# Hybrid decoder layer in fp32 on one core: half 0's seven-product stages with rounded part and remainder side by side

## The chip, the cores and the metric

The kernel runs on one core of a Trainium2 chip. The metric is the device time of one execution in microseconds; lower is better. The median of three runs of the kernel before is 2952.33 us (2952.29 to 2953.47).

## What is computed

One layer of a hybrid decoder trunk, for 1024 prompt tokens and 64 sample tokens of width 1024: two half-step SwiGLU feed-forward networks (FFN1, FFN2) around a token mixer (a pooling branch and a Mamba-2 SSD branch, merged by gates), then a final norm. All in fp32.

```
def swiglu(x, w_in, w_out):
    gu = x @ w_in
    g, u = gu[..., :D_FF], gu[..., D_FF:]
    return (jax.nn.silu(g) * u) @ w_out

x = x + 0.5 * swiglu(rmsnorm(x, norm_ffn1), ffn1_w_in, ffn1_w_out)
mix, ... = token_mixing(rmsnorm(x, norm_mix), ...)
x = x + mix
x = x + 0.5 * swiglu(rmsnorm(x, norm_ffn2), ffn2_w_in, ffn2_w_out)
```

D_MODEL is 1024 and D_FF is 2816. The change concerns `x @ w_in` of both FFNs.

## The kernel before

Tokens lie along the columns and channels on the 128 partitions. They are split into half 0 (512 tokens) and half 1 (576 tokens, the samples among them). An fp32 product is made from three products of a rounded type (fp32r): an operand is split into its rounded part (`hi`, `xh`, `wh`) and the remainder (`lo`, `xl`, `wl`), and wh·xh + wh·xl + wl·xh is summed in PSUM. ScalarE rounds, VectorE subtracts (`split`, L350 and L352 for activations; L455 and L456, or L289 and L290, for weights).

**Input product of an FFN.** It goes through 22 blocks `ff` of 128 channels of g and 128 of u. The first blocks (3 for half 0, 2 for half 1: `N_PLAIN`) are made plainly. The others (`ffn_in`, `wino`) use a Strassen-Winograd scheme: g and u for two groups of tokens are a 2 x 2 block product over two halves of the 1024 input channels, which takes seven products rather than eight. Each product has 4 K tiles of 128 and a width of 256 columns in half 0 or 288 in half 1. `combine` makes its operands: those of products 1, 2 and 3 are slices of the normed, split tiles `hi` and `lo`; those of 4 to 7 are sums, split by `put` (tiles `X`, the rounded part in columns 0 to n, the remainder next to it; for product 4 into a part of `hi` and `lo` that is no longer used). `wino_weights` makes the seven weight operands: four raw tiles, four sums s1 to s4 on GpSimd (L449), each split into wh and wl.

The products run in the order 1, 2, 6, 5, 7, 3, 4 and gather in three PSUM banks a half: A takes 1, 6, 7, 4 (each added to what lies there), B takes 2, C takes 5 and 3. `after` takes out what is needed after each product, with ScalarE copies (L548, L556, L558), VectorE adds (L553, L560, L562) and a multiply (L565), two SiLUs on ScalarE (L554, L563) and a multiply on GpSimd (L566). There are six such banks, so the next block's A, B and C are the same banks. In blocks 3 to 20 each product is made for half 0 and then for half 1 with the same weights ("joint" blocks, 18 in each FFN); block 2 is half 1's alone; block 21 (`N_APART`) is made for half 0 alone and then for half 1 alone. The result of a block is stored to DRAM (`hd`, L567).

**Output product.** For each half the 22 stored tiles come back (`hr`, L629), are split into `hh` and `hr`, and are multiplied with `w_out` in 8 blocks of output channels (`po`). All 22 tiles stay in SBUF for the half.

**What sets the order.** The program is written as generators that are stepped by due times on a model clock of TensorE; a tile framework adds the waits and chooses the order on each engine by priority. Weight splits and sums have a raised priority (`hp`). SyncE issues nearly all DMAs, in order: a load whose buffer is not free holds back those behind it. Activation tiles of [128, 576] come from a pool of 58 (`act`) and, in the FFNs, from one of 17 (`fx`).

Of the kernel before, what the change touches and what calls it, by code (L numbers as in the profile page):

```python
# [8 lines left out]
F32 = mybir.dt.float32  # L9
# [5 lines left out]
P = 128  # L15
# [47 lines left out]
def tile_hybrid_pool_ssd_macaron(  # L63
# [340 lines left out]
    def norm_split(xt, h, gi, out, pace=1.0):  # L404

        N = NTOK[h]
        rr = []
        yield from rstd(xt, h, D, rr, pace)
        hi, lo = [], []
        for k in range(KD):  # L410
            a = act((P, N), F32R, "hi")
            b = act((P, N), F32R, "lo")
            t = act((P, N), name="xn")
            V.tensor_tensor(t, xt[k], rr[0], op=ALU.mult)
            split(t, a, b, cols[:, gi + k : gi + k + 1])
            hi.append(a)
            lo.append(b)
            yield pace
        out.append((h, hi, lo))
# [59 lines left out]
    def wino(weights, nk, xs, after):  # L479


        banks = [[None] * 3 for _ in xs]
        for (p, b), (wh, wl) in zip(PRODUCTS, weights):
            for i, (h, X) in enumerate(xs):
                n = NPAIR[h]
                new = banks[i][b] is None
                if new:
                    banks[i][b] = psum("pd", "pw" + p)
                out = banks[i][b][:, :n]
                for k in range(nk):  # L490
                    xh, xl = X[p][k]
                    for j, (W, x) in enumerate(((wh, xh), (wh, xl), (wl, xh))):
                        mm(out, W[:, k, :], x, start=new and k == 0 and j == 0, stop=k == nk - 1 and j == 2, free=True)
                after(p, i, banks[i])
                tick()

    def combine(h, xn, hi, lo, X, pace):

        n = NPAIR[h]
        f, s_ = slice(0, n), slice(n, 2 * n)
        X["1"] = [(hi[i][:, f], lo[i][:, f]) for i in range(4)]
        X["2"] = [(hi[4 + i][:, f], lo[4 + i][:, f]) for i in range(4)]
        X["3"] = [(hi[4 + i][:, s_], lo[4 + i][:, s_]) for i in range(4)]
        for p in "6574":
            X[p] = []

        def sub(out, a, b):
            G.tensor_tensor(out, a, b, op=ALU.subtract)  # L510

        def put(src, p, a=None, b=None):
            if a is None:
                t = act((P, 576), F32R, "X")
                a, b = t[:, f], t[:, s_]
            S.activation(a, src, AF.Copy)
            V.tensor_tensor(b, src, a.bitcast(F32), op=ALU.subtract)
            X[p].append((a, b))

        for i in range(4):  # L520
            a, b = xn[i], xn[4 + i]
            sub(a[:, s_], a[:, s_], a[:, f])
            t2 = fx(name="t2")[:, f]
            sub(t2, b[:, s_], a[:, s_])
            put(t2, "6")
            put(a[:, s_], "5")
            yield pace
            sub(a[:, f], t2, a[:, f])
            sub(b[:, f], b[:, f], t2)
            put(a[:, f], "7")  # L530
            yield pace
        yield None
        for i in range(4):
            put(xn[4 + i][:, f], "4", hi[i][:, s_], lo[i][:, s_])
            yield pace

    def ffn_in(wi, ff, xs):

        out = {}

        def after(p, i, bk):
            h = xs[i][0]
            n = NPAIR[h]
            A, B, C = (b[:, :n] if b is not None else None for b in bk)
            if p == "1":
                t = fx(name="t")
                out[i] = o = {"g": fx(name="g"), "t1": t[:, :n], "t5": t[:, :n], "t2": t[:, n : 2 * n]}
                S.copy(o["t1"], A)  # L548
                return
            o = out[i]  # L550
            g1, g2 = o["g"][:, :n], o["g"][:, n : 2 * n]
            if p == "2":
                V.tensor_tensor(g1, B, o["t1"], op=ALU.add)  # L553
                S.activation(g1, g1, AF.Silu)  # L554
            elif p == "6":
                S.copy(o["t2"], A)  # L556
            elif p == "5":
                S.copy(o["t5"], C)  # L558
            elif p == "7":
                V.tensor_tensor(o["t5"], A, o["t5"], op=ALU.add)  # L560
            elif p == "3":
                V.tensor_tensor(g2, C, o["t2"], op=ALU.add)  # L562
                S.activation(g2, g2, AF.Silu)  # L563
            else:
                V.tensor_tensor(g1, g1, A, op=ALU.mult)  # L565
                G.tensor_tensor(g2, g2, o["t5"], op=ALU.mult)  # L566
                dma(hdram[h][ff], o["g"][:, : 2 * n])  # L567

        wino(wino_weights(wi, 0, 4, 4, ff * P, FF + ff * P), 4, xs, after)
# [17 lines left out]
    def ffn(wi, wo, prep, after, half=None, side=None):  # L587
# [33 lines left out]
        for h in HALVES:  # L621
            N = NTOK[h]
            parts = [], []
            for k in range(NFF):

                own = k < 4 if h == 0 else not half and k >= NFF - 2
                t, a = (fx(d, n_) if own else act((P, 576), d, n_) for d, n_ in ((F32, "hr"), (F32R, "hh")))
                t = t[:, :N]
                dma(t, hdram[h][k])  # L629
                split(t, a[:, :N], t.bitcast(F32R))  # L630
# [35 lines left out]
    def load_x(h, out):  # L666
# [37 lines left out]
        hi, lo, xn = [None] * KD, [None] * KD, [None] * KD  # L704
        for k in range(KD):
            pt = psum("ps", "ptx")
            for i in range(4):
                mm(pt[:, i * P : (i + 1) * P], raws[i][k // 4][:, (k % 4) * P : (k % 4 + 1) * P], dg[i])
            x = fx(name="xn") if k >= 4 else act((P, 576), name="xn")
            a, b = act((P, 576), F32R, "hi"), act((P, 576), F32R, "lo")  # L710
            g = cols[:, i_g1 + k : i_g1 + k + 1]
            S.activation(x[:, :512], pt, AF.Copy, scale=g)
            V.tensor_scalar_mul(a[:, :512], pt, g)
# [5 lines left out]
            hi[k], lo[k], xn[k] = a, b, x  # L719
            yield 0.9  # L720
        out.append((h, hi, lo, xn))

    def turn_x(h):

# [15 lines left out]
    def norm_parts(xt, h, gi, out, pace=1.0):  # L740

        N = NTOK[h]
        rr = []
        yield from rstd([t[:, :N] for t in xt], h, D, rr, pace)
        hi, lo, xn = [], [], []
        for k in range(KD):
            x = fx(name="xn") if k >= 4 else act((P, 576), name="xn")
            a, b = act((P, 576), F32R, "hi"), act((P, 576), F32R, "lo")
# [6 lines left out]
        out.append((h, hi, lo, xn))  # L755


    ch, hn = {}, []
# [798 lines left out]
```

## Time and profile before

| | |
|---|---|
| median of three runs | 2952.33 us |
| span of the profiled execution | 2950.3 us (its own time lies some 2.0 us above, taken from the median) |
| TensorE busy | 2900.3 us (98%), 19740 matmuls |
| VectorE / ScalarE / GpSimd busy | 1646.5 us (56%) / 1187.0 us (40%) / 445.1 us (15%) |
| matmuls of half 0's seven-product blocks (`pw`, 256 columns) | 608 x 3 on `hi`, `lo`; 912 + 456 on `X` |
| FFN1's seven-product stage | about 106 to 529 us of the span |

In a profile row the engine, the line, the operation and the tiles (out<-in) are followed by the shape; groups have count, busy time in us, mean ns of one, and the idle time ahead with what ended it. A window row has its bounds, its length, busy us and count of PE, PEld, DVE, ACT and POOL, then the granted clock, the DMA share and GB/s. PE is TensorE, DVE VectorE, ACT ScalarE, POOL GpSimd, SP SyncE.

### The profile page before, as it was taken

Reading aid. Unit: us, or ns where it says so; the run is one execution under the profiler, and the core shown is the slowest. Engines: PE = TensorE matmul, PEld = TensorE weight load, DVE = VectorE, ACT = ScalarE, POOL = GpSimd, SP = SyncE. Lnnn points to the kernel's source line nnn. Section 1 sums busy time; section 2 is a strip of 40 time slices with the busy share of each in tenths; the row PEclk is TensorE's granted clock in tenths of the full one; section 3 lists DMA queues with packets and bytes.
Section 4 is the critical chain, followed back from the end, with each engine's and each line's share of the span. In section 5 each row is a group of like instructions: output and inputs, shape, how many; then the busy total and the mean of one; then the engine's idle time right before and its main releaser. Section 6 shows DMA issues by size and latency. Waiting matters only on the chain. (4 is left out here: it accounts for less than half of the span.)

```text
span 2950.3 us, 52088 instructions
## 1 busy us (share of the span) xinstructions
PE 2900.3 (98%) x19740; PEld 2689.1 (91%) x19740; DVE 1646.5 (56%) x3134; ACT 1187.0 (40%) x2418; POOL 445.1 (15%) x528
## 2 busy tenths in 40 slices
PE   7999999999999999999999999999999999999998
PEld 6999999789988888788999988999999999997898
DVE  5654445434273897777633776867665443443432
ACT  5444444333242665443332454442333433342322
POOL 5433333000000000000000010100034333330000
PEclk9999999999999999999999999999999999999999
DMA  4465554864335888678434566556574522236652
GB/s 131 155 220 176 164 161 152 271 201 142 101 98 168 276 258 265 196 225 286 118 97 152 170 184 183 168 155 186 178 240 155 165 90 76 79 106 203 197 179 72
DMA packets 542273, 501.36 MB, mean 170 GB/s; under 512 B 36388, under 2 KB 391780, under 8 KB 542014
## 3 DMA queue, kind: packets, MB, share of 16 engines
q1 hardware_dynamic: 542006, 498.03, 54.0%
q8 instruction: 155, 2.54, 0.4%
q14 instruction: 96, 0.79, 0.1%
q10 hardware_dynamic: 16, 0.00, 0.0%
HBM read 355.94 MB, written 142.20 MB: 169 GB/s over the span
## 5 line engine op out<-in xcount | busy, mean ns | idle before, releaser
L290 DVE TENSOR_TENSOR wl<-wraw,wh 128x512 fp32r<-128x512 f32 (+1 forms) x416 | 282.8, 681 | 394.7 <-ACT wh L289 386.6
L289 ACT ACTIVATE wh<-wraw 128x512 fp32r<-128x512 f32 (+1 forms) x416 | 256.4, 617 | 603.0 <-PE po L161 233.7
L161 PE MATMUL pw<-hi,wh 128*128 128x288 f32 (+1 forms) x1248 | 361.3, 289 | 2.6 <-DVE t L560 2.2
L161 PE MATMUL pw<-hi,wl 128*128 128x288 f32 (+1 forms) x1248 | 360.1, 289 | 0.0
L161 PE MATMUL pw<-lo,wh 128*128 128x288 f32 (+1 forms) x1248 | 359.9, 288 | 0.0
L161 PE MATMUL pw<-X,wh 128*128 128x288 f32 (+1 forms) x1872 | 356.9, 289 | 0.2 <-ACT t L556 0.2
L161 PEld LDWEIGHTS pw<-X,wh 128*128 128x128 f32 x1872 | 295.8, 190 | 0.4 <-ACT t L556 0.4
L161 PE MATMUL po<-hh,wh 128*128 128x288 f32 (+1 forms) x1056 | 288.1, 330 | 6.8 <-ACT hh L350 6.6
L161 PE MATMUL po<-hr,wh 128*128 128x288 f32 (+1 forms) x1056 | 289.4, 328 | 0.0
L161 PE MATMUL po<-hh,wl 128*128 128x288 f32 (+1 forms) x1056 | 288.6, 328 | 0.0
L161 PE MATMUL pw<-X,wl 128*128 128x288 f32 (+1 forms) x936 | 270.1, 289 | 0.0
L161 PEld LDWEIGHTS pw<-hi,wh 128*128 128x128 f32 x1248 | 236.2, 189 | 3.5 <-DVE t L560 2.6
L161 PEld LDWEIGHTS pw<-lo,wh 128*128 128x128 f32 x1248 | 236.1, 189 | 0.0
L161 PEld LDWEIGHTS pw<-hi,wl 128*128 128x128 f32 x1248 | 236.1, 189 | 0.0
L456 DVE TENSOR_TENSOR wl<-s,wh 128x512 fp32r<-128x512 f32 x168 | 123.4, 736 | 145.3 <-ACT wh L455 142.2
L161 PEld LDWEIGHTS po<-hh,wh 128*128 128x128 f32 x1056 | 179.0, 189 | 24.3 <-ACT hh L350 11.1
L161 PEld LDWEIGHTS po<-hr,wh 128*128 128x128 f32 x1056 | 179.9, 189 | 15.8 <-DVE hr L352 2.3
L161 PEld LDWEIGHTS po<-hh,wl 128*128 128x128 f32 x1056 | 180.0, 189 | 14.2 <-DMA wl<-part 0.4
L161 PEld LDWEIGHTS pw<-X,wl 128*128 128x128 f32 x936 | 178.1, 190 | 0.0
L455 ACT ACTIVATE wh<-s 128x512 fp32r<-128x512 f32 x168 | 106.2, 632 | 174.4 <-PE pw L161 170.7
L161 PE MATMUL pc<-hi,wh 128*128 128x288 f32 (+1 forms) x576 | 161.5, 334 | 0.0
L161 PE MATMUL pc<-lo,wh 128*128 128x288 f32 (+1 forms) x576 | 158.2, 328 | 0.0
(341 smaller groups left out, 6391.0 us busy)
## 6 DMA issues: line engine op xcount, KB each, us to landing
wh<-part SPq DMA_DIRECT2D x204, 256.0 KB
wl<-part SPq DMA_DIRECT2D x204, 256.0 KB
wraw<-in_ffn_w_in_dram SPq DMA_DIRECT2D x188, 256.0 KB
wraw<-in_w_in_dram SPq DMA_DIRECT2D x180, 256.0 KB
wraw<-in_ffn_w_out_dram SPq DMA_DIRECT2D x120, 256.0 KB
part<-wh SPq DMA_DIRECT2D x112, 256.0 KB
part<-wl SPq DMA_DIRECT2D x112, 256.0 KB
ab<-acsd SPq DMA_DIRECT2D x64, 256.0 KB
```

The costliest lines, as they stand in the source:

```text
L161: T.matmul(out, lhsT, rhs, start=start, stop=stop, skip_group_check=free)
L289: S.activation(wh, raw, AF.Copy)
L290: V.tensor_tensor(wl, raw, wh.bitcast(F32), op=ALU.subtract)
L455: S.activation(wh, a, AF.Copy)
L456: V.tensor_tensor(wl, a, wh.bitcast(F32), op=ALU.subtract)
```

## The change

Half 0's operands get a layout in which the rounded part and the remainder lie in one tile: `pair` gives [128, 2, 576], eight of them, and the pool of act tiles shrinks from 58 to 42. `X` tiles are read as two pieces of 256 columns. For half 0, `wino` makes per K tile one matmul of 512 columns with wh on both pieces, into a whole bank, and one of 256 with wl on the rounded part, into the bank's first half. The two halves of a bank are thus two parts of one sum; `after0` takes them out side by side (copies and adds of 512 columns) and sums them on GpSimd (`halves`), or for product 4 with a ScalarE copy of the second half and a VectorE add. A third fx tile `v` is used per block. Half 1 is computed as before. The pairs also hold the mixer norm's `hi` and `lo` (`norm_split`) and, in the output stage, tiles 4 to 11 of half 0 (and of half 1 in FFN2).

```diff
...
 PIECES = (((0, 512),), ((0, 288), (288, 576)), ((0, 256),), ((256, 576),))
 HALF_OF = (0, 1, 1, 1)
 NPAIR = (256, 288)
-N_ACT, N_BIG, N_PD = 58, 3, 4
+N_ACT, N_PAIR, N_BIG, N_PD = 42, 8, 3, 4
 N_RAW, N_W = 6, 3
 N_FX, N_S, N_PDF = 17, 4, 6
 N_PLAIN, N_APART = (3, 2), 1
...
     def act(shape=(P, 576), dt=F32, name="a"):
         return sp.tile(list(shape), dt, tag="act", bufs=N_ACT, name=nm(name))
+    def pair(n, name="hl"):
+        t = sp.tile([P, 2, 576], F32R, tag="pair", bufs=N_PAIR, name=nm(name))
+        return t[:, 0, :n], t[:, 1, :n], t
     stage = {}
...
         yield from rstd(xt, h, D, rr, pace)
         hi, lo = [], []
         for k in range(KD):
-            a = act((P, N), F32R, "hi")
-            b = act((P, N), F32R, "lo")
+            a, b, _ = pair(N)
             t = act((P, N), name="xn")
             V.tensor_tensor(t, xt[k], rr[0], op=ALU.mult)
             split(t, a, b, cols[:, gi + k : gi + k + 1])
...
                 if new:
                     banks[i][b] = psum("pd", "pw" + p)
                 out = banks[i][b][:, :n]
+                if h == 0:
+                    both = banks[i][b].rearrange("p (a b) -> p a b", a=2)
+                    for k in range(nk):
+                        x = X[p][k]
+                        mm(both, wh[:, k, :], x, start=new and k == 0, stop=False, free=True)
+                        mm(out, wl[:, k, :], x[:, 0, :], start=False, stop=k == nk - 1, free=True)
+                    after(p, i, banks[i])
+                    tick()
+                    continue
                 for k in range(nk):
                     xh, xl = X[p][k]
                     for j, (W, x) in enumerate(((wh, xh), (wh, xl), (wl, xh))):
...
                 after(p, i, banks[i])
                 tick()
-    def combine(h, xn, hi, lo, X, pace):
+    def combine(h, xn, hi, lo, hl, X, pace):
         n = NPAIR[h]
         f, s_ = slice(0, n), slice(n, 2 * n)
-        X["1"] = [(hi[i][:, f], lo[i][:, f]) for i in range(4)]
-        X["2"] = [(hi[4 + i][:, f], lo[4 + i][:, f]) for i in range(4)]
-        X["3"] = [(hi[4 + i][:, s_], lo[4 + i][:, s_]) for i in range(4)]
+        for p, i0, cs in (("1", 0, f), ("2", 4, f), ("3", 4, s_)):
+            X[p] = [(hi[i0 + i][:, cs], lo[i0 + i][:, cs]) if h else hl[i0 + i][:, :, cs] for i in range(4)]
         for p in "6574":
             X[p] = []
...
             G.tensor_tensor(out, a, b, op=ALU.subtract)
         def put(src, p, a=None, b=None):
+            both = None
             if a is None:
                 t = act((P, 576), F32R, "X")
                 a, b = t[:, f], t[:, s_]
+                both = t[:, : 2 * n].rearrange("p (a b) -> p a b", a=2)
             S.activation(a, src, AF.Copy)
             V.tensor_tensor(b, src, a.bitcast(F32), op=ALU.subtract)
-            X[p].append((a, b))
+            X[p].append((a, b) if h else both)
         for i in range(4):
             a, b = xn[i], xn[4 + i]
...
         yield None
         for i in range(4):
             put(xn[4 + i][:, f], "4", hi[i][:, s_], lo[i][:, s_])
+            if h == 0:
+                X["4"][i] = hl[i][:, :, s_]
             yield pace
     def ffn_in(wi, ff, xs):
         out = {}
+
+        def after0(p, i, bk):
+
+            A, B, C = bk
+            n = NPAIR[0]
+            f, s_ = slice(0, n), slice(n, 2 * n)
+            if p == "1":
+                out[i] = o = {"g": fx(name="g"), "t": fx(name="t"), "v": fx(name="v")}
+                S.copy(o["t"][:, : 2 * n], A)
+                return
+            g, t, v = out[i]["g"], out[i]["t"], out[i]["v"]
+
+            def halves(o, x):
+                G.tensor_tensor(o, x[:, f], x[:, s_], op=ALU.add)
+
+            if p == "2":
+                V.tensor_tensor(g[:, : 2 * n], B, t[:, : 2 * n], op=ALU.add)
+                halves(g[:, f], g)
+                S.activation(g[:, f], g[:, f], AF.Silu)
+            elif p == "6":
+                S.copy(v[:, : 2 * n], A)
+            elif p == "5":
+                S.copy(t[:, : 2 * n], C)
+            elif p == "7":
+                V.tensor_tensor(t[:, : 2 * n], A, t[:, : 2 * n], op=ALU.add)
+                halves(t[:, f], t)
+            elif p == "3":
+                V.tensor_tensor(v[:, : 2 * n], C, v[:, : 2 * n], op=ALU.add)
+                halves(g[:, s_], v)
+                S.activation(g[:, s_], g[:, s_], AF.Silu)
+            else:
+                S.copy(t[:, s_], A[:, s_])
+                V.tensor_tensor(t[:, s_], A[:, f], t[:, s_], op=ALU.add)
+                V.tensor_tensor(g[:, f], g[:, f], t[:, s_], op=ALU.mult)
+                G.tensor_tensor(g[:, s_], g[:, s_], t[:, f], op=ALU.mult)
+                dma(hdram[0][ff], g[:, : 2 * n])
         def after(p, i, bk):
             h = xs[i][0]
+            if h == 0:
+                return after0(p, i, bk)
             n = NPAIR[h]
             A, B, C = (b[:, :n] if b is not None else None for b in bk)
             if p == "1":
...
         for h in HALVES:
             finish(prep[h][0])
             x = prep[h][1][0]
-            gen = combine(h, x[3], x[1], x[2], X[h], T_PACE)
+            gen = combine(h, x[3], x[1], x[2], x[4], X[h], T_PACE)
             def first(gen):
                 for p in gen:
...
             for k in range(NFF):
                 own = k < 4 if h == 0 else not half and k >= NFF - 2
-                t, a = (fx(d, n_) if own else act((P, 576), d, n_) for d, n_ in ((F32, "hr"), (F32R, "hh")))
+                if 4 <= k < 4 + N_PAIR and (h == 0 or half):
+                    a, t, _ = pair(576, "hp")
+                    t = t.bitcast(F32)
+                else:
+                    t, a = (fx(d, n_) if own else act((P, 576), d, n_) for d, n_ in ((F32, "hr"), (F32R, "hh")))
                 t = t[:, :N]
                 dma(t, hdram[h][k])
                 split(t, a[:, :N], t.bitcast(F32R))
...
         N = NTOK[h]
         rr = []
         yield from rstd([t[:, :N] for t in xt], h, D, rr, pace)
-        hi, lo, xn = [], [], []
+        hi, lo, xn, hl = [], [], [], []
         for k in range(KD):
             x = fx(name="xn") if k >= 4 else act((P, 576), name="xn")
-            a, b = act((P, 576), F32R, "hi"), act((P, 576), F32R, "lo")
+            a, b, both = (act((P, 576), F32R, "hi"), act((P, 576), F32R, "lo"), None) if h else pair(576)
             V.scalar_tensor_tensor(x[:, :N], xt[k][:, :N], cols[:, gi + k : gi + k + 1], rr[0], op0=ALU.mult, op1=ALU.mult)
             split(x[:, :N], a[:, :N], b[:, :N])
             hi.append(a)
             lo.append(b)
             xn.append(x)
+            hl.append(both)
             yield pace
     ch, hn = {}, []
```

In the rows below, a name is followed by its tile's number. **TensorE, product 1 of half 0 in a joint block of FFN1, and the first matmuls of half 1.** Before:

```order
L161 MATMUL pw1_579_3118<-hi_46_281,wh_577_3114 128x256
L161 MATMUL pw1_579_3118<-lo_47_282,wh_577_3114 128x256
L161 MATMUL pw1_579_3118<-hi_46_281,wl_578_3115 128x256
L161 MATMUL pw1_579_3118<-hi_50_292,wh_577_3114 128x256
L161 MATMUL pw1_579_3118<-lo_51_293,wh_577_3114 128x256
L161 MATMUL pw1_579_3118<-hi_50_292,wl_578_3115 128x256
L161 MATMUL pw1_579_3118<-hi_54_303,wh_577_3114 128x256
L161 MATMUL pw1_579_3118<-lo_55_304,wh_577_3114 128x256
L161 MATMUL pw1_579_3118<-hi_54_303,wl_578_3115 128x256
L161 MATMUL pw1_579_3118<-hi_58_314,wh_577_3114 128x256
L161 MATMUL pw1_579_3118<-lo_59_315,wh_577_3114 128x256
L161 MATMUL pw1_579_3118<-hi_58_314,wl_578_3115 128x256
```

After:

```order
L164 MATMUL pw1_588_2998<-hl_46_281,wh_586_2994 128x512
L164 MATMUL pw1_588_2998<-hl_46_281,wl_587_2995 128x256
L164 MATMUL pw1_588_2998<-hl_49_291,wh_586_2994 128x512
L164 MATMUL pw1_588_2998<-hl_49_291,wl_587_2995 128x256
L164 MATMUL pw1_588_2998<-hl_52_301,wh_586_2994 128x512
L164 MATMUL pw1_588_2998<-hl_52_301,wl_587_2995 128x256
L164 MATMUL pw1_588_2998<-hl_55_311,wh_586_2994 128x512
L164 MATMUL pw1_588_2998<-hl_55_311,wl_587_2995 128x256
L164 MATMUL pw1_592_3011<-hi_89_437,wh_586_2994 128x288
```

Of three matmuls for each K tile two are left, the first of 512 columns; half 1 follows as before.

**ScalarE at the boundary between two joint blocks** (`wh` are weight splits of the next block's first products; `g` SiLUs; `pw1` is bank A, `pw5` bank C). Before:

```order
L455 ACTIVATE wh_577_3114<-wraw_573_3106 128x512
L563 ACTIVATE g_531_2837<-g_531_2837 128x256
L455 ACTIVATE wh_585_3154<-wraw_574_3108 128x512
L563 ACTIVATE g_534_2853<-g_534_2853 128x288
L455 ACTIVATE wh_596_3199<-s2_595_3197 128x512
L735 COPY xr_465_2514<-ptr_571_3095 128x64
L735 COPY xr_467_2516<-ptr_571_3095 128x64
L548 COPY t_580_3131<-pw1_579_3118 128x256
L455 ACTIVATE wh_598_3229<-s1_594_3195 128x512
L548 COPY t_583_3147<-pw1_582_3134 128x288
```

After:

```order
L457 ACTIVATE wh_586_2994<-wraw_582_2986 128x512
L353 ACTIVATE ph_577_2979<-pr_574_2931 128x512
L457 ACTIVATE wh_595_3027<-wraw_583_2988 128x512
L583 ACTIVATE g_537_2745<-g_537_2745 128x256
L615 ACTIVATE g_542_2763<-g_542_2763 128x288
L585 COPY t_538_2746<-pw1_536_2736 128x256
L457 ACTIVATE wh_602_3064<-s2_601_3062 128x512
L562 COPY t_590_3008<-pw1_588_2998 128x512
```

Between half 1's SiLU (L615) and the copy for product 1 of the next block (L562) there is now a copy of a part of bank A after product 4 (L585). On VectorE an add and a multiply (L586, L587) stand where the multiply L565 stood.

**GpSimd over the same block** (`s1` to `s4` are weight sums of the next block). Before:

```order
L449 TENSOR_TENSOR s1_594_3195<-wraw_575_3110,wraw_576_3112 128x512
L449 TENSOR_TENSOR s2_595_3197<-s1_594_3195,wraw_573_3106 128x512
L449 TENSOR_TENSOR s3_603_3263<-wraw_573_3106,wraw_575_3110 128x512
L449 TENSOR_TENSOR s4_611_3302<-wraw_574_3108,s2_595_3197 128x512
L566 TENSOR_TENSOR g_531_2837<-g_531_2837,t_530_2836 128x256
L566 TENSOR_TENSOR g_534_2853<-g_534_2853,t_533_2852 128x288
```

After:

```order
L451 TENSOR_TENSOR s1_600_3060<-wraw_584_2990,wraw_585_2992 128x512
L451 TENSOR_TENSOR s2_601_3062<-s1_600_3060,wraw_582_2986 128x512
L567 TENSOR_TENSOR g_537_2745<-g_537_2745 128x256
L451 TENSOR_TENSOR s3_613_3125<-wraw_582_2986,wraw_584_2990 128x512
L451 TENSOR_TENSOR s4_617_3156<-wraw_583_2988,s2_601_3062 128x512
L567 TENSOR_TENSOR t_538_2746<-t_538_2746 128x256
L567 TENSOR_TENSOR g_537_2745<-v_539_2747 128x256
L588 TENSOR_TENSOR g_537_2745<-g_537_2745,t_538_2746 128x256
L618 TENSOR_TENSOR g_542_2763<-g_542_2763,t_541_2762 128x288
```

The three sums of bank halves (L567) stand between the weight sums and ahead of the closing multiplies (L588, L618).

**SyncE at the transition from FFN1's input to its output product** (`hr` and `hp` loads of stored tiles, whose number follows `hd0_`; `wh`, `wl` weights; `hd0_21`, `hd1_21` the stores of the last blocks). Before, from tile 8 of half 0 on:

```order
L629 DMA hr_1188_6607<-hd0_8_129 128x512
L629 DMA hr_1172_6567<-hd0_0_121 128x512
L629 DMA hr_1190_6612<-hd0_9_130 128x512
L629 DMA hr_1174_6572<-hd0_1_122 128x512
L279 DMA wh_1220_6695<-part_436_2309 128x512
L629 DMA hr_1192_6617<-hd0_10_131 128x512
L629 DMA hr_1176_6577<-hd0_2_123 128x512
L279 DMA wl_1221_6697<-part_438_2310 128x512
L279 DMA wh_1224_6727<-part_455_2427 128x512
L567 DMA hd1_21_164<-g_1153_6449 128x576
L629 DMA hr_1178_6582<-hd0_3_124 128x512
L629 DMA hr_1194_6622<-hd0_11_132 128x512
```

After, from tile 8 on:

```order
L685 DMA hp_1195_6177<-hd0_8_129 128x512
L685 DMA hp_1196_6181<-hd0_9_130 128x512
L589 DMA hd0_21_142<-g_1135_5896 128x512
L685 DMA hr_1183_6141<-hd0_0_121 128x512
L685 DMA hp_1197_6185<-hd0_10_131 128x512
L685 DMA hp_1198_6189<-hd0_11_132 128x512
L685 DMA hr_1205_6208<-hd0_15_136 128x512
L282 DMA wl_1226_6279<-part_319_1645 128x512
L685 DMA hr_1185_6146<-hd0_1_122 128x512
L282 DMA wh_1223_6261<-part_425_2182 128x512
L685 DMA hr_1207_6213<-hd0_16_137 128x512
L282 DMA wl_1224_6263<-part_427_2183 128x512
```

And on to tile 3:

```order
L685 DMA hr_1187_6151<-hd0_2_123 128x512
L282 DMA wh_1227_6293<-part_444_2279 128x512
L619 DMA hd1_21_164<-g_1164_6023 128x576
L685 DMA hr_1209_6218<-hd0_17_138 128x512
L685 DMA hr_1189_6156<-hd0_3_124 128x512
```

Tiles 4 to 9 (in the pairs) stand ahead of tile 0, and tiles 15, 16 and 17 have come between tiles 0 and 3. The number of DMAs is the same.

More of the change, by code (lines that the diff above doesn't have):

```diff
@@ L718, in load_x @@
             (G if k % 2 else V).tensor_tensor(b[:, :N], x[:, :N], a[:, :N].bitcast(F32), op=ALU.subtract)
-            hi[k], lo[k], xn[k] = a, b, x
+            hi[k], lo[k], xn[k], hl[k] = a, b, x, both
             yield 0.9
-        out.append((h, hi, lo, xn))
+        out.append((h, hi, lo, xn, hl))
     def turn_x(h):
@@ L744, in norm_parts @@
         yield from rstd([t[:, :N] for t in xt], h, D, rr, pace)
-        hi, lo, xn = [], [], []
+        hi, lo, xn, hl = [], [], [], []
         for k in range(KD):
             x = fx(name="xn") if k >= 4 else act((P, 576), name="xn")
-            a, b = act((P, 576), F32R, "hi"), act((P, 576), F32R, "lo")
+            a, b, both = (act((P, 576), F32R, "hi"), act((P, 576), F32R, "lo"), None) if h else pair(576)
             V.scalar_tensor_tensor(x[:, :N], xt[k][:, :N], cols[:, gi + k : gi + k + 1], rr[0], op0=ALU.mult, op1=ALU.mult)
@@ L753, in norm_parts @@
             xn.append(x)
+            hl.append(both)
             yield pace
-        out.append((h, hi, lo, xn))
+        out.append((h, hi, lo, xn, hl))
     ch, hn = {}, []
```

2 lines of the change are left out of this document (1 added, 1 removed).

## The prediction

> **What bounds the kernel now.** I read the page first, then the waits of TensorE, the windows over the seven-product stage, the groups by shape, and last the timeline at the places that the change touches. From the page:
>
> ```profile
> span 2950.3 us, 52088 instructions
> PE 2900.3 (98%) x19740; PEld 2689.1 (91%) x19740; DVE 1646.5 (56%) x3134; ACT 1187.0 (40%) x2418; POOL 445.1 (15%) x528
> ```
>
> TensorE is busy for 98% of the span, and no other engine for more than 56%. Some 2.0 us of the 2952.33 us median lie around this span, so sums made against the span can be put on the median. The seven-product stage of FFN1 in one window, and TensorE's longest waits that lie at the change:
>
> ```profile
> 106.00:506.00 400.00, 399.79 (x3175) 399.09 (x3175) 199.44 (x358) 177.76 (x395) 139.81 (x113) 1.00 0.55 175
> PE po L161 <- ACT hh L350: 6.6, 7, 1.8
> PE pw L161 <- DVE t L560: 2.2, 2, 1.1
> ```
>
> In 400 us TensorE stands still for 0.2 us, at a granted clock of 1.00; VectorE is busy for half of it, ScalarE for 44%, GpSimd for 35%. So in this stage time goes down only when TensorE's own stream gets shorter, and up only when a new wait appears. The waits of the output product `po` (6.6 us) lie at the transition to it, and the 2.2 us of `pw` are two stalls in the block that half 0 has for itself.
>
> **The merged matmuls (the gain).** What is removed:
>
> ```profile
> L161 PE MATMUL pw<-hi,wh 128*128 128x256 f32 x608 | 172.3, 283 | 2.2 <-DVE t L560 2.2
> L161 PE MATMUL pw<-hi,wl 128*128 128x256 f32 x608 | 171.7, 282 | 0.0
> L161 PE MATMUL pw<-X,wh 128*128 128x256 f32 x912 | 168.9, 283 | 0.0
> L161 PE MATMUL pw<-X,wl 128*128 128x256 f32 x456 | 129.0, 283 | 0.0
> ```
>
> The mean of one is a latency, for neighbours overlap; the price is the distance between starts. Half 0 has 38 blocks of 7 products of 4 K tiles: 1064 K tiles (608 on norm tiles and 456 on `X` tiles, as the counts show), each with two 256-column matmuls on `wh`. These two become one of 512 columns, so 1064 matmuls go, each with its weight load. Starts from the timeline: two whole half-0 products (12 matmuls of 256 columns each, up to the first of half 1), the next block's first matmul, and 512-column matmuls of the output stage, 23 steps apart.
>
> ```profile
> 312.81 0.28 PE L161 MATMUL pw<-hi,wh 128*128 128x256 f32 x1
> ...
> 314.23 0.30 PE L161 MATMUL pw<-hi,wh 128*128 128x288 f32 x1
> ...
> 315.83 0.28 PE L161 MATMUL pw<-hi,wh 128*128 128x256 f32 x1
> ...
> 318.83 0.28 PE L161 MATMUL pw<-hi,wh 128*128 128x256 f32 x1
> ...
> 320.27 0.30 PE L161 MATMUL pw<-hi,wh 128*128 128x288 f32 x1
> ...
> 2674.68 0.39 PE L161 MATMUL po<-hh,wl 128*128 128x512 f32 x1
> ...
> 2679.89 0.39 PE L161 MATMUL po<-hr,wh 128*128 128x512 f32 x1
> ```
>
> A product takes 314.23 - 312.81 = 1.42 or 320.27 - 318.83 = 1.44 us, so a 256-column matmul 118 to 120 ns. A 512-column one takes 5.21 / 23 = 226.5 ns. A merge saves 2 x 118.3 - 226.5 = 10 to 2 x 120 - 226.5 = 13.5 ns, which is 10.7 to 14.4 us for 1064; I take 12.5 ns (most steps in the timeline are 120): **-13.3 us**. The 512-column row has one contiguous operand and the new one reads two 256-column pieces that lie 576 columns apart (for `X` they touch). No row shows such a read; a gain from it is excluded, and the loss reaches from nothing to the whole saving. I take nothing, since the rows price a matmul by its columns: 288 of them cost (315.83 - 314.23) / 12 = 133 ns, above 256 by what the columns say.
>
> Here the Trainium skill speaks against the change: the page "TensorE: Matmul & The Clock Gate", section "Back-to-back issue gap", gives a warm gap of N / 2.4 + 2.5 ns, so only 2.5 ns are fixed per matmul and the merges would bring an estimated 2.7 us. The rows put the fixed part at some 12 ns (120 ns at 256 columns, 226.5 at 512), and I go by them.
>
> **Leaving PSUM.** Per half-0 block ScalarE's three copies and VectorE's two adds double in width, ScalarE and VectorE get one more 256-column operation each, and GpSimd three adds of 256 columns. Nearest rows, and GpSimd's multiply of the same size:
>
> ```profile
> L548 ACT COPY t<-pw 128x256 f32<-128x256 f32 x38 | 14.1, 372 | 28.3 <-PE pw L161 28.1
> L815 ACT COPY craw<-pc 128x512 f32<-128x512 f32 x24 | 13.8, 576 | 0.1
> L560 DVE TENSOR_TENSOR t<-pw,t 128x256 f32<-128x256 f32 x38 | 16.0, 422 | 4.2 <-PE pw L161 3.5
> L1264 DVE TENSOR_TENSOR hst<-hst,pst 128x512 f32<-128x512 f32 x28 | 19.1, 681 | 0.7 <-PE pst L161 0.3
> 312.37 0.74 POOL L566 TENSOR_TENSOR g<-g,t 128x256 f32<-128x256 f32 x1 [5.17 <-ACT g L563]
> ```
>
> ScalarE gets 3 x (576 - 372) + 372 = 984 ns more per block, VectorE 3 x (681 - 422) + 422 = 1.2 us (its third add was in width 256 too), GpSimd 3 x 0.74 = 2.2 us. A joint block lasts 7 x (1.42 + 1.60) = 21 us, of which each is busy for half or less, so their sums cost nothing; only latency to TensorE's next use of a bank can. Banks: A is written by products 1, 6, 7, 4 in this order, C by 5 and 3, B by 2. In between, each copy has the other half's product and two more (1.6 + 1.4 + 1.6 us or so), against 0.58 or 0.68 for the operation. The tight one is bank A after product 4: only half 1's product 4 (1.60 us) lies before the next block writes A. Before, one multiply frees it:
>
> ```profile
> 314.02 0.93 POOL L566 TENSOR_TENSOR g<-g,t 128x288 f32<-128x288 f32 x1 [0.91 <-ACT g L563]
> 314.43 0.42 DVE L565 TENSOR_TENSOR g<-g,pw 128x256 f32<-128x256 f32 x1 [0.15 <-PE pw L161]
> ```
>
> It ends at 314.85, 0.98 us ahead of 315.83. After, a copy (0.37) and an add (0.42) stand in its place, with a handover of about 0.15 between engines (the idle in the row above): 314.43 + 0.37 + 0.15 + 0.42 = 315.37, 0.46 us ahead. GpSimd's 0.93 us ran beside this VectorE operation without stretching it. ScalarE holds two SiLUs and a weight split ahead of the copy, and the first SiLU now waits for GpSimd's sum; from product 3's end I count 0.15 + 0.68 (add) + 0.74 (sum), then 0.63 + 0.42 + 0.45 on ScalarE, which is 3.1 us, just where product 4 ends (1.60 + 1.40). So I put **0** here, with 0.4 us of cover.
>
> **Half 0's own block** (the last in each FFN). With no half-1 products between, a product is 1.4 us away from the next use of its bank. Before, it lost 1.1 us ahead of product 4:
>
> ```profile
> 507.90 1.29 POOL L449 TENSOR_TENSOR s<-wraw,wraw 128x512 f32<-128x512 f32 x1 [2.52 <-DVE wl L456]
> 509.89 1.30 POOL L449 TENSOR_TENSOR s<-s,wraw 128x512 f32<-128x512 f32 x1 [0.70 <-DVE wl L456]
> 516.13 0.39 PE L161 MATMUL pw<-hi,wh 128*128 128x256 f32 x1 [1.08 <-DVE t L560]
> ```
>
> After, GpSimd's first sum stands behind the two weight sums of the next block, which end at 511.19. Then follow the sum 0.74, the SiLU 0.42, a weight split 0.63 and the copy of A 0.58 on ScalarE: 513.6, while product 7 could begin at about 506.3 + 4 x 1.38 = 511.8. That is a stall of 1.8 us in place of one of about 1.1 to 1.2, which then has time to pass unseen: +0.6 us for each FFN, bounds 0 and +2, together **+1.2**.
>
> **Transition to the output product.** SyncE issues loads in order. Tiles 4 to 11 of half 0 now lie in the pairs and so can be loaded only when products 3 and 4 of half 0's last block are done, and six of them stand ahead of tile 0; tiles 12 to 17 come ahead of tile 3. In the trace tile 3 is what TensorE waits for:
>
> ```profile
> 529.61 0.32 SPq L567 DMA_DIRECT2D hd<-g  x1
> 529.98 0.93 SPq L629 DMA_DIRECT2D hr<-hd  x2
> 535.33 0.50 PE L161 MATMUL po<-hh,wh 128*128 128x512 f32 x1 [1.64 <-ACT hh L350]
> 2666.89 0.80 PE L161 MATMUL po<-hh,wh 128*128 128x512 f32 x2 [1.84 <-ACT hh L350]
> 523.00:526.00 3.00, 3.00 (x24) 2.93 (x24) 2.62 (x5) 2.74 (x7) 0.00 (x0) 1.00 0.53 192
> 526.00:529.00 3.00, 3.00 (x24) 3.00 (x24) 2.07 (x5) 1.42 (x3) 0.37 (x1) 1.00 0.67 226
> 532.00:535.00 3.00, 1.70 (x8) 1.04 (x6) 0.00 (x0) 0.35 (x1) 0.00 (x0) 1.00 0.86 278
> 2660.60:2671.20 10.60, 8.76 (x31) 6.27 (x30) 3.78 (x6) 2.68 (x5) 0.58 (x2) 0.84 0.91 296
> ```
>
> The load of tile 3 is issued behind the store of half 1's last block (529.61) both before and after, now with one more load between: 0.4 us of issue, and 256 KB more at 278 GB/s, 0.9 us. Some seven loads are moved ahead of it in all; the DMA engines were used to 0.53 and 0.67 there, so about half of these find room, and the others would delay it by up to 3 x 0.9 us. I take +1.3 us for each FFN. The stall of 1.84 us in FFN2 is followed by a half clock: 10.60 us at a mean of 0.84 cost 10.60 x 0.16 = 1.7 us; the 1.64 us stall in FFN1 is not. A longer one there gets it by about even chance, 0.9 us. Together **+3.5**, bounds -1 (the later tiles being there already can take away later stalls) and +9.
>
> The mixer norm also moves into pairs; its half 1 starts after half 0's last use, so nothing waits. The start of FFN1 is ordered a little differently around `ptx`, for which I put 0 with 3 us either way.
>
> **The sum.** -13.3 + 1.2 + 3.5 = -8.6 us: 2952.3 - 8.6 = **2943.7 us**. What a measurement of this kernel can tell from no change is about 0.2%, 5.9 us: faster is below 2946.4, slower above 2958.2.
>
> **Rivals.**
> *Bank A comes free too late (slower).* If the chain from the end of product 4 to the add's end is over 1.60 us, each of the 36 boundaries between a joint block and the next stalls. By the count above 0.4 us are left. If GpSimd's sum, or the SiLU behind it, comes 0.9 us late (two weight sums of 1.3 us can stand ahead of it), 0.5 us of stall come of it: 36 x 0.5 = 18 us, 2961.7 us. For it: the chain now crosses VectorE, GpSimd, ScalarE and VectorE again. Against it: weight sums stand early in a block, and the 0.93 us GpSimd row did not stretch VectorE. Chance 0.11.
> *The merge brings nothing.* A matmul that reads two pieces takes as long as the two that it replaces, 240 ns: 2952.3 + 4.7 = 2957.0 us. Against it stands the price by columns in every contiguous row; nothing in the trace shows two pieces. Chance 0.07. The Trainium skill's rule above ("TensorE: Matmul & The Clock Gate", "Back-to-back issue gap") comes out beside this case.
> *The output stage takes it back.* Tiles 0 to 3 all come late, with a half clock in both FFNs: 3 us and 1.7 us more in each than I put, less what is in the sum, some +7: 2951 us. For it: the DMA share of 0.86 and more there. Chance 0.11.
> *The start of FFN1* or another reordering moves over 3 us either way: chance 0.03.
> The forecast keeps 0.68.
>
> **How the numbers follow.** The likeliest case alone reaches from 2938 (gain 14.4, no losses) to 2949 (gain 10.7, losses 7.4). With the output-stage rival and part of the no-gain case the range is 2937.5 to 2955; the bank rival and the rest lie outside. Faster takes 0.61 of the forecast's 0.68 and 0.01 of the start's: 0.62. Within 0.2% lie 0.07 of the forecast, the output-stage rival's 0.11 and 0.05 of the no-gain case: 0.23. Slower takes the bank rival's 0.11, and 0.02 each of no gain and of the start: 0.15.
>
> **What would show it.** Starts of 512-column `pw` matmuls 227 ns apart followed by 120 (a half-0 product in 1.39 us); no wait of `pw` for an add or copy of bank A between blocks, one of about 1.8 us ahead of product 7 in each lone block; `po` waiting for tiles 0 to 3 by 1 to 2 us more. A row of `pw` waiting in x36, or 240 ns between starts, would make the prediction wrong.

## The result and the profile after

| | before | after |
|---|---|---|
| median | 2952.31 us (2948.60 to 2953.47, 6 runs) | 2941.18 us (2938.48 to 2945.62, 6 runs) |
| ratio | | 0.9969, 95% interval 0.9959 to 0.9979 |
| profiled execution | span 2950.3 us | 2938.48 us, span 2936.7 us |

The change made the kernel 11.1 us faster; 8.6 us were forecast. The profiled execution of after is the fastest of its six, so the 13.6 us between the two spans are some 2.5 us more than the medians differ by. From the page of after, then TensorE's waits in `pw` and `po`:

```profile
span 2936.7 us, 50272 instructions
PE 2887.0 (98%) x18676; PEld 2628.6 (90%) x18676; DVE 1702.4 (58%) x3172; ACT 1206.3 (41%) x2456; POOL 531.0 (18%) x642
PE pw L164 <- ACT v L574: 3.8, 3, 1.8
PE po L164 <- ACT hh L353: 3.2, 4, 1.0
PE pw L164 <- ACT t L610: 1.2, 1, 1.2
```

There are 1064 matmuls fewer, as counted. The waits of `po` halved from 6.6 us, and a wait of `pw` for ScalarE's copy `v` is new. Where the 13.6 us lie follows from the starts of TensorE's matmuls at seven places of both traces:

| from the place before up to | before, us | after, us | change in the stretch |
|---|---|---|---|
| first `pw` of FFN1 | 105.96 | 101.83 | -4.1 |
| end of half 0's products, FFN1 | 517.54 | 511.64 | -1.8 |
| first `po` of half 1, FFN1 | 653.95 | 647.51 | -0.5 |
| first `pw` of half 0, FFN2 | 2256.52 | 2250.80 | +0.7 |
| end of half 0's products, FFN2 | 2648.69 | 2640.70 | -2.3 |
| first `po` of half 1, FFN2 | 2789.75 | 2777.57 | -4.2 |
| last matmul | 2937.17 | 2923.56 | -1.4 |

Only 4.1 us come from the two stretches that hold the merged matmuls. Two half-0 products of joint blocks of after, each from its first matmul to half 1's first:

```profile
301.24 0.40 PE L164 MATMUL pw<-X,wh 128*128 128x512 f32 x1
...
302.62 0.29 PE L164 MATMUL pw<-X,wh 128*128 128x288 f32 x1
...
316.12 0.40 PE L164 MATMUL pw<-X,wh 128*128 128x512 f32 x1
316.36 0.28 PE L164 MATMUL pw<-X,wl 128*128 128x256 f32 x1
316.48 0.39 PE L164 MATMUL pw<-X,wh 128*128 128x512 f32 x1
...
317.54 0.30 PE L164 MATMUL pw<-X,wh 128*128 128x288 f32 x1
```

They take 1.38 and 1.42 us. Over FFN2 the medians are 1.424 to 1.437 us before (10.03 us for the seven) and after 1.387 (products 1, 7, 3, 4), 1.397 (2), 1.407 (5) and 1.413 (6), 9.77 us. That is 0.265 us for 28 K tiles, **9.5 ns a merge, 10.1 us in all** if FFN1's merges are worth the same. The rest of the gain there was given back. In FFN1's lone block, which half 0 has for itself (ScalarE, then TensorE):

```profile
505.85 0.42 ACT L572 ACTIVATE g<-g 128x256 f32<-128x256 f32 x1 [2.58 <-POOL g L567]
506.20 0.63 ACT L457 ACTIVATE wh<-s 128x512 fp32r<-128x512 f32 x1
506.73 0.57 ACT L574 COPY v<-pw 128x512 f32<-128x512 f32 x1
507.36 0.50 PE L164 MATMUL pw<-X,wh 128*128 128x512 f32 x1 [1.84 <-ACT v L574]
```

The SiLU waits 2.58 us for GpSimd's sum, a weight split follows, then the copy that frees bank A, and product 7 waits 1.84 us, as forecast. FFN2's lone block waits 1.76 us at the same place, and behind it the clock is granted at half:

```profile
2634.95 0.51 PE L164 MATMUL pw<-X,wh 128*128 128x512 f32 x1 [1.76 <-ACT v L574]
...
2637.95 0.63 PE L164 MATMUL pw<-hl,wh 128*128 128x512 f32 x1
2638.38 0.41 PE L164 MATMUL pw<-hl,wl 128*128 128x256 f32 x1
```

```profile
2632.00:2641.00 9.00, 7.24 (x34) 5.97 (x33) 7.12 (x9) 4.84 (x10) 5.79 (x6) 0.81 0.50 179
```

Starts are 430 ns apart after 512 columns, not 232. At a mean clock of 0.81 over 9 us this costs 9.0 x 0.19 = 1.7 us. The Trainium skill ("TensorE: Matmul & The Clock Gate", its part on the HAM clock gate) says that this gate is only ever at full or at half; these starts agree. At the transitions to the output product (SyncE, TensorE, and windows of after):

```profile
510.03 2.76 SPq L685 DMA_DIRECT2D hp<-hd  x6
...
526.03 0.73 PE L164 MATMUL po<-hh,wh 128*128 128x512 f32 x2 [0.96 <-ACT hh L353]
...
531.51 0.73 PE L164 MATMUL po<-hh,wh 128*128 128x512 f32 x2 [0.96 <-ACT hh L353]
...
2659.13 0.74 PE L164 MATMUL po<-hh,wh 128*128 128x512 f32 x2 [0.76 <-ACT hh L353]
```

```profile
511.00:514.00 3.00, 3.00 (x23) 2.91 (x22) 3.00 (x4) 1.38 (x3) 1.44 (x2) 1.00 0.98 323
520.00:523.00 3.00, 3.00 (x22) 2.77 (x22) 3.00 (x6) 3.00 (x7) 0.00 (x0) 1.00 0.99 367
523.00:526.00 3.00, 2.07 (x14) 1.60 (x12) 2.04 (x5) 1.16 (x3) 1.31 (x1) 1.00 1.01 338
```

And the first of these windows before:

```profile
511.00:514.00 3.00, 3.00 (x27) 3.00 (x27) 2.53 (x4) 2.48 (x6) 2.37 (x3) 1.00 0.17 64
```

Six loads into the pairs are issued from 510.03 on, before half 0's products end. The DMA engines are then at 0.98 where they had been at 0.17, and are full up to the transition, where they had been at 0.53 and 0.67. TensorE's stalls there are under 1 us each, and the half clock that followed FFN2's stall is gone.

### The profile page after: what moved, and what is told of

The parts are those of the page before. It is cut to its first block, busy times and chain, and to the rows that moved or that the text cites. A ratio compares the mean times of both kernels' runs of the same rounds, so it can differ in the third digit from the quotient of the medians.

```text
span 2936.7 us, 50272 instructions
## 1 busy us (share of the span) xinstructions
PE 2887.0 (98%) x18676; PEld 2628.6 (90%) x18676; DVE 1702.4 (58%) x3172; ACT 1206.3 (41%) x2456; POOL 531.0 (18%) x642
## 5 line engine op out<-in xcount | busy, mean ns | idle before, releaser
L164 PE MATMUL pc<-hl,wh 128*128 128x288 f32 (+1 forms) x1152 | 257.0, 330 | 0.0
L164 PE MATMUL pw<-hl,wh 128*128 128x512 f32 x608 | 220.4, 397 | 0.0
L458 DVE TENSOR_TENSOR wl<-s,wh 128x512 fp32r<-128x512 f32 x168 | 129.9, 774 | 146.4 <-ACT wh L457 124.9
L164 PE MATMUL pg<-hl,wh 128*128 128x288 f32 (+1 forms) x864 | 201.6, 338 | 0.8 <-issue 0.8
L164 PEld LDWEIGHTS pc<-hl,wh 128*128 128x128 f32 x1152 | 184.0, 188 | 18.9 <-issue 4.2
L164 PE MATMUL pw<-hi,wh 128*128 128x288 f32 x640 | 189.1, 295 | 1.2 <-ACT t L610 1.2
L164 PE MATMUL pw<-hi,wl 128*128 128x288 f32 x640 | 188.4, 294 | 0.0
L164 PE MATMUL pw<-lo,wh 128*128 128x288 f32 x640 | 188.4, 294 | 0.0
L164 PE MATMUL pz<-hl,wh 128*128 128x288 f32 (+1 forms) x768 | 172.2, 333 | 0.0
L164 PE MATMUL pw<-hl,wl 128*128 128x256 f32 x608 | 169.7, 279 | 0.0
L164 PE MATMUL pc<-hl,wl 128*128 128x288 f32 (+1 forms) x576 | 157.6, 327 | 0.0
```

The costliest lines, as they stand in the source:

```text
L164: T.matmul(out, lhsT, rhs, start=start, stop=stop, skip_group_check=free)
L458: V.tensor_tensor(wl, a, wh.bitcast(F32), op=ALU.subtract)
```

## The experiments

Each kernel is the changed one with the edit shown; times are medians, ratios are to the kernel before on the same chip.

**The changed kernel again** (`after_again`).

> The changed kernel itself, for comparison on one chip. 2941 us, within 3 us. A wait of about 1.8 us ahead of product 7 in each of half 0's lone blocks again (it is a fixed queue order), a half-0 product in joint blocks at 1.39 to 1.41 us. If the 4.2 us that the first profile gained ahead of the seven-product stage of FFN1 are chance, that stretch will differ by some us here; if they come from the order of instructions there, the first `pw` will stand at about 101.8 us again.

2941.17 us (8 runs), ratio 0.9970 (0.9960 to 0.9980). The first `pw` stands at 102.05 us. The longest wait of `po` is 1.72 us here, in FFN1, against 0.96 in the first profile. Both lone blocks wait 1.8 us again, and this time both have the half clock behind it; from FFN1's:

```profile
507.00:511.00 4.00, 4.00 (x16) 3.37 (x15) 3.95 (x5) 1.58 (x4) 2.07 (x2) 0.57 0.75 236
```

**The kernel before again** (`before_again`).

> The kernel before, once more, for its profile. Theory (the 4.1 us that all profiles with the new layout gain ahead of FFN1's seven-product stage, and the shorter stalls of the output stages, come of the order of instructions): first `pw` at about 106 us again, `po` stalls of about 2 us at tile 3. Rival (chance of the one profile): first `pw` near 102 us.

2948.61 us, one run. The first `pw` lies at 104.37 us, between the two expectations: in the nine profiles with the new layout it lies at 101.4 to 103.6 us, in the two without it at 104.4 and 106.0. So the start's gain is not chance alone, but the 4.1 us of the first profile are its upper end; 1.6 us of difference between runs of one kernel stand there too. FFN1's stall at tile 3 is back, with a half clock behind it:

```profile
PE po L161 <- ACT hh L350: 5.5, 7, 1.9
530.00:545.00 15.00, 13.09 (x49) 9.89 (x50) 3.50 (x6) 3.16 (x5) 0.00 (x0) 0.89 0.83 281
```

**The layout without the merge** (`layout_only`): `wino` and `after` for half 0 as before the change, the pairs kept.

```diff
-                if h == 0:
-                    both = banks[i][b].rearrange("p (a b) -> p a b", a=2)
...
-            if h == 0:
-                return after0(p, i, bk)
```

> The pairs, the smaller act pool and the output stage's use of the pairs stay; half 0's products are three matmuls of 256 columns again and leave PSUM as before the change. Theory (the merge saves 9.5 ns for each of 1064 K tiles, the layout saves some 6 us by loads at the transitions to the output products, the lone blocks lose some 3 us by the new summing): slower than the changed kernel by 10.1 - 3 = 7 us, about 2948; half-0 product 1.43 us, lone blocks with 1.2 us stalls, first stalls of `po` as short as after the change. Rival (the layout and the order do it all): as fast as the changed kernel, 2941 or less. Rival (the merge does it all): 2952.

2945.69 us (11 runs), ratio 0.9988 (0.9979 to 0.9997). The layout alone gains 5.2 us by the medians (3.5 by the ratio), and the merge with its summing 4.5 more, where the theory had 7. Neither rival holds. Its half-0 product takes 1.437 us, its `po` waits are short, and its lone blocks have the old stall (waits of TensorE):

```profile
PE po L164 <- ACT hh L353: 2.2, 2, 1.5
PE pw L164 <- DVE t L599: 2.2, 2, 1.1
```

So the transitions were mended by the layout, with the loads as it orders them, and not by the merge.

**The sum of bank B on VectorE** (`sum_dve`).

```diff
-                halves(g[:, f], g)
+                V.tensor_tensor(g[:, f], g[:, f], g[:, s_], op=ALU.add)
```

> The sum of bank B's halves after product 2 on VectorE rather than GpSimd. Theory (in the lone block the SiLU, and behind it the copy of bank A, waits for GpSimd's sum behind two weight sums): the wait ahead of product 7 falls from 1.8 us to under 0.8 us in both FFNs and with it the half clock behind it in FFN2 (1.6 us): 2 to 4 us faster than the changed kernel, joint blocks unchanged. Rival (the copy waits for the weight split of s4 or for VectorE anyway): the wait stays at 1.5 us or more, no change.

2936.63 us (5 runs), ratio 0.9957 (0.9944 to 0.9969): 4.5 us below the changed kernel by the medians, a little over what was expected. The wait ahead of product 7 falls to 1 us, not below 0.8, and the half clocks behind it are gone:

```profile
504.29 0.42 ACT L572 ACTIVATE g<-g 128x256 f32<-128x256 f32 x1 [0.89 <-DVE g L571]
504.61 0.57 ACT L574 COPY v<-pw 128x512 f32<-128x512 f32 x1
505.23 0.50 PE L164 MATMUL pw<-X,wh 128*128 128x512 f32 x1 [0.97 <-ACT v L574]
```

The weight split stands ahead of the SiLU now; what is left is the SiLU, whose sum waits on VectorE.

Laid beside `layout_only`, whose wait in each lone block is about as long (1.1 us, 1.0 here), this run shows the merge by itself. The stretch from half 0's first `pw` to half 1's first `pw` behind half 0's products runs from 113.86 to 513.26 and from 2250.59 to 2642.87 us in `layout_only`, from 114.29 to 509.51 and from 2250.68 to 2637.80 us here. It is 4.2 us shorter in FFN1 and 5.2 in FFN2. Half 0's matmuls are 5.0 and 5.2 us shorter, as 9.5 ns a merge asks for; in FFN1 half 1's took 0.8 us more, which is not explained.

**Tiles 0 to 7 in the pairs** (`pairs_first`), with fx tiles for 8 to 11.

```diff
-                own = k < 4 if h == 0 else not half and k >= NFF - 2
-                if 4 <= k < 4 + N_PAIR and (h == 0 or half):
+                own = 8 <= k < 12 if h == 0 else not half and k >= NFF - 2
+                if (k < N_PAIR if h == 0 else half and 4 <= k < 4 + N_PAIR):
```

> In the output stage of half 0 the pairs hold tiles 0 to 7, and the fx tiles hold 8 to 11, so tiles 0 to 3 stand first in SyncE's queue. Theory (the remaining stalls of `po` come of tiles 0 to 3 standing behind six other loads): the first stalls of `po` (some 2.3 us in FFN1, 2.5 in FFN2) go, 2 to 5 us faster than the changed kernel. Rival (the DMA engines, busy at 0.95 to 1.0 from half 0's last product on, are the bound): the stalls move to tiles 8 to 11, within 1 us of the changed kernel.

2939.33 us (5 runs), ratio 0.9965 (0.9953 to 0.9978), 1.8 us below the changed kernel, which the intervals do not tell apart. The trace is plainer: no wait of `po` for `hh` is left among TensorE's waits. The window behind FFN1's transition (first `po` at 525.71):

```profile
525.00:540.00 15.00, 14.89 (x69) 12.12 (x68) 6.80 (x11) 5.39 (x9) 1.28 (x1) 1.00 0.98 344
```

In the first 15 us from the first `po` on TensorE was busy 14.89 us in FFN1 and 14.80 in FFN2, against 12.95 and 13.25 in after, with the DMA engines at 0.99 to 1.01 in all four. So the DMA engines were not the bound: what the queue brings first was. From the first `po` to half 1's first `po` it took 121.35 and 122.70 us, against 123.29 and 125.64, 4.9 us less, inside the 2 to 5 that were expected. The medians show less of it, partly because half 1's output stage in FFN2 took 147.45 us here and 145.99 in after.

**A longer way out of bank A** (`long_chain`).

```diff
-                S.copy(t[:, s_], A[:, s_])
+                for _ in range(4):
+                    S.copy(t[:, s_], A[:, s_])
```

> The changed kernel with ScalarE's copy of bank A's second half after product 4 made four times, so that bank A comes free some 1.1 to 1.3 us later. The trace of the changed kernel has 0.57 us between the end of the add that frees it and the next block's first matmul. Theory (bank A is the tight one, with 0.5 us of cover): a stall of 0.5 to 0.8 us ahead of product 1 at each of 36 boundaries, 18 to 29 us more, 2959 to 2970. Rival (another wait or a longer cover decides): under 5 us more.

2948.31 us (8 runs), ratio 0.9994 (0.9983 to 1.0004): 7 us above the changed kernel. That is over the rival's 5 but far from 18, and none of it lies at the block boundaries. ScalarE, TensorE and VectorE at one of them:

```profile
2316.70 1.59 ACT L586 COPY t<-pw 128x256 f32<-128x256 f32 x4
2318.10 0.40 PE L164 MATMUL pw<-hl,wh 128*128 128x512 f32 x1
2318.32 0.42 DVE L587 TENSOR_TENSOR t<-pw,t 128x256 f32<-128x256 f32 x1 [1.22 <-ACT t L586]
```

The next block's first matmul begins at 2318.10, while bank A is read until 2318.74. So the next block does not write this bank first. The numbers of the banks in the compiled program show it: three blocks in a row hold A, B, C of half 0 in banks (4, 3, 7), (3, 7, 4), (7, 4, 3), before the change as after. Banks are handed out in the order in which they are freed, and A's goes to the next block's C, which is first written three products of each half later. (That the next block's banks are the same, as the description of the kernel above says, holds for the three of a half together, not one by one.) The loss arises elsewhere. This profile is 6.0 us longer than the first one of the changed kernel, and 5.7 us of that lie between the end of half 0's products and half 1's first `po` (2.7 in FFN1, 3.0 in FFN2), where half clocks follow `po` stalls of 1.67 and 1.54 us. Why those stalls grew is open. The wait for `v` in the lone blocks grew to 2.2 us, with no half clock behind it.

**Order within a product** (`wh_first`).

```diff
-                        mm(out, wl[:, k, :], x[:, 0, :], start=False, stop=k == nk - 1, free=True)
+                    for k in range(nk):
+                        mm(out, wl[:, k, :], X[p][k][:, 0, :], start=False, stop=k == nk - 1, free=True)
```

> The changed kernel with the order within a half-0 product changed: first the four matmuls of 512 columns with wh, then the four of 256 with wl. In the changed kernel a start after a 512-column matmul comes 232 ns later and one after a 256-column matmul 117 ns, 349 ns a K tile, and products last 1.387, 1.397, 1.407 or 1.413 us by which product it is. If going from 512 to 256 columns is what costs 5 ns more than 512 after 512 (226.5), a product has it once rather than four times: 3 x 226.5 + 232 + 4 x 119 = 1.388 us, all products near there, 1 to 2 us less in all. Rival (the product's tiles set it, not the order): the same durations by product as before, no change in time.

2944.21 us (10 runs), ratio 0.9975 (0.9966 to 0.9985), no gain. In FFN2 half-0 products last 1.398 to 1.409 us, against 1.387 to 1.413; the seven add up to 9.84 us, against 9.77. The median from one 512-column start to the next is 233 ns, as it was to a 256-column one. So the changeover is not what costs 5 ns. Nor is the rival right as stated: the durations by product changed with the order.

**Both mends** (`both`: `sum_dve` with `pairs_first`) and **one SiLU** (`one_silu_pairs`: `pairs_first`, the sum on GpSimd, and one SiLU of 512 columns after product 3).

```diff
                 halves(g[:, f], g)
-                S.activation(g[:, f], g[:, f], AF.Silu)
...
-                S.activation(g[:, s_], g[:, s_], AF.Silu)
+                S.activation(g[:, : 2 * n], g[:, : 2 * n], AF.Silu)
```

> The sum after product 2 on VectorE, and tiles 0 to 7 of half 0's output stage in the pairs. If the two gains are apart from each other: 4.5 us and some 2 to 4 us below the changed kernel, 2933 to 2936. If they share a stall: 2937.

> Tiles 0 to 7 in the pairs as before; the sum after product 2 is on GpSimd again, and one SiLU of 512 columns after product 3 takes the place of the two of 256, so nothing on ScalarE stands ahead of the copy of bank A after product 6 that waits for GpSimd. Theory (that SiLU is what holds the copy): the wait ahead of product 7 falls under 0.6 us, 0.5 to 1 us for each FFN below the version with the sum on VectorE and the same loads. Rival (the weight split of s4 holds it): as long as there, 1.0 us.

2933.70 us, ratio 0.9943 (0.9930 to 0.9955), and 2931.95 us, ratio 0.9938 (0.9924 to 0.9951), 5 runs each. The first is 7.5 us below the changed kernel, a little more than the two gains together (4.5 and 1.8 us). The second is the fastest kernel here, 18.5 us below the kernel before. Its only waits of `pw` that come to over 0.5 us in total:

```profile
PE pw L164 <- ACT t L599: 2.5, 2, 1.3
PE pw L164 <- DVE t L577: 0.7, 2, 0.4
```

The wait ahead of product 7 is gone; a new one of 0.4 us for VectorE stands before product 4 instead, and half 1's lone block waits 1.3 us for a copy behind the splits of loaded tiles. That the SiLU, waiting for GpSimd, had held bank A's copy is thereby shown. The 1.8 us between the two versions are within their intervals.

## Why the prediction was right, step by step

The sign and the size were right, but the sum was right through misses that cancel: the merge brought 3 us less than forecast and half clocks took up to 3.4 us more, while the transitions came out 8 us better and the start up to 4 us better. That the total came near is in part luck.

- **What bounds the kernel** held: TensorE is busy 98% of a shorter span, and the 19 to 86 us more of work on the other engines cost little in joint blocks: the longest wait in the first profile is 1.2 us in FFN1 (`t`, L610), in the second 0.6 us in FFN2 (`v`).
- **The merged matmuls**: forecast 12.5 ns each, 13.3 us, bounds from 10 ns; measured 9.5 ns, 10.1 us, just under the bound. The mis-sized term is the 512-column matmul: 232 ns in this stage, where the output stage's row gave 226.5. The 256-column matmul behind it took 117 ns, not 120, which gives back about half of that. Two pieces are not the reason: matmuls on `X`, whose pieces touch, and on `hl` have the same median, 233 and 232 ns. Why this stage is slower by 5 ns stays open. The Trainium skill ("TensorE: Matmul & The Clock Gate", "Back-to-back issue gap") gives N / 2.4 + 2.5 ns for a matmul by itself, by which the merges would bring an estimated 2.7 us. For a stream with a weight load to each matmul, as here, it gives 131 ns at 512 columns instead, which the prediction did not weigh. The 232 ns of this stage agree with neither, and the runs decide.
- **Leaving PSUM**: 0 in joint blocks was right for a wrong reason. The 0.46 us of cover at bank A does not exist, because the next block begins in another bank; the cover is several products. The rival built on it could not have come true, as `long_chain` shows.
- **Half 0's own block**: place, cause and wait (1.8 us) were as worked out; +0.7 us each against +0.6. The term missed the half clock that can follow such a stall, 1.7 us, in FFN2 of one profile and in both FFNs of the other.
- **The transition to the output product** is the step that failed: forecast +3.5 us, lower bound -1; measured -0.5 in FFN1 and -4.2 in FFN2. Between the second profiles of both kernels it is -4.0 and -0.7, so -4.7 together each time; the larger part falls where the kernel before had its half clock. I took the seven loads moved ahead of tile 3 to delay it. Six were issued from 510.03 on, into a stretch in which the DMA engines had been idle for most of the time (0.17 from 511 to 514 us), probably because loads stood in the queue behind weight loads that waited for a buffer (this was not tried by itself); so they cost tile 3 little, and the later stalls and FFN2's half clock went too.
- **The start of FFN1**: 0 with 3 either way; the first profile had -4.1, the pairs of profiles -0.8 to -4.6. The layout did this, not the merge, since the plain blocks there are not merged and `layout_only` has it too (101.39 us).

Of the merge's 10.1 us the changed kernel keeps less than half: the two stretches with the merged matmuls are 4.2 us shorter in its first profile and 3.6 in its second than in `layout_only`, and it is 4.5 us faster than that by the medians. The rest went into longer waits, half clocks, and half 1's matmuls in FFN1. `sum_dve`, without most of those losses, is 9 us faster than `layout_only`. The layout's 3.5 to 5.2 us make up the rest of the gain. That FFN2's half-1 output stage ran 1.4 us faster, with no stall in either trace that tells them apart, is not explained: it takes 146.0 us in the six profiles with tiles 4 to 11 of half 0 in the pairs, about 147.5 in the three with tiles 0 to 7, and 147.4 and 146.4 in the two of the kernel before.

## What to carry to other kernels

Widening a matmul pays for each weight load and matmul that goes, here 9.5 ns; take the price from the stage itself and not from another one. Before counting the cover of a buffer, look up which buffer the allocator hands out next: a rotating pool gives what was freed first, not the one of the same role. A sum put on an idle engine joins that engine's queue; where an in-order engine waits for it, everything behind that wait is late too, and the stall can cost twice when the clock drops behind it.

## What the runs showed of the hardware

A stall of about 1.8 us of TensorE was followed by some 3.4 us of half clock (1.7 us lost) in some executions and not in others: at one and the same place (FFN1's lone block) it came in one profile of the changed kernel and not in the other, and behind the 2.2 us stalls of `long_chain` at this place it did not come either. Stalls of 1.54 and 1.67 us of `po` had it there. At 1 to 1.25 us ahead of product 7 or 4 it did not come in any profile here. VectorE was stretched beside GpSimd in the lone blocks: a weight remainder on VectorE, 0.69 us while GpSimd was idle, took 1.28 and 1.45 us beside GpSimd's sums (VectorE, then GpSimd):

```profile
500.64 0.69 DVE L458 TENSOR_TENSOR wl<-s,wh 128x512 fp32r<-128x512 f32 x1 [0.21 <-ACT wh L457]
501.98 1.28 DVE L458 TENSOR_TENSOR wl<-s,wh 128x512 fp32r<-128x512 f32 x1 [0.64 <-ACT wh L457]
503.78 1.45 DVE L458 TENSOR_TENSOR wl<-s,wh 128x512 fp32r<-128x512 f32 x1
501.41 1.30 POOL L451 TENSOR_TENSOR s<-wraw,wraw 128x512 f32<-128x512 f32 x1 [1.96 <-DVE wl L458]
503.39 1.30 POOL L451 TENSOR_TENSOR s<-s,wraw 128x512 f32<-128x512 f32 x1 [0.68 <-POOL s L451]
```
